# A convolution tile on GpSimd without its place behind the first norm's squares, and kept weights loaded through two buffer rings

## Chip, cores and metric

One core of a Trainium2 chip runs the whole kernel. The metric is device time in microseconds (us) of one execution; before the change the median of three runs is 753.43 us (753.04 to 754.24).

## What is computed

Two layers on a sequence of 1024 tokens of width 1024, in float32 (cut from the reference):

```
layer 0:  h = rms(x, g0) * (1 + sc) + sh
          a, b, g = split(h @ cv_w_in, 3);   y = a * sigmoid(b)
          y = depthwise_conv31(y) + db
          y = silu(layernorm(y)) * silu(g);  x = x + gt * (y @ cv_w_out)
layer 1:  h = rms(x, g1) * (1 + sc) + sh
          v, g = split(h @ pl_w_in, 2)
          y = (window_mean(v) - v) @ w_grp * scale          # four groups, windows 2, 4, 8, 16
          x = x + gt * ((y * silu(g)) @ pl_w_out)
```

`sh`, `sc` and `gt` of each layer come from `silu(c) @ w_mod`. The context prefix has no effect on the output at this depth and is left out.

## The kernel before

Everything is held transposed: 128 channels on the partitions, tokens along the free axis. The sequence is worked in two halves of 512 tokens (h = 0 and 1), the channels in eight tiles of 128 (ct = 0 to 7). Each matrix product is made from three matmuls (`mm3`, lines 217 to 219): operand and weight are each split into a rounded high part and the rest, and high times high, high times low and low times high are added. One product of a 128x1024 weight with a half is 24 matmuls of 128x512.

**How a weight arrives.** `load_split` (L193) loads 512 KB into a buffer of the ring "raw", ScalarE (ACT) writes the high part (L166), VectorE (DVE) or GpSimd (POOL) the low part (L171); both parts go to two buffers of the ring "w" unless slots are named. A raw buffer is free again as soon as the low part is written. Both rings have four buffers of the same size (L63). While layer 0's gates are computed, `split_ahead` (L557) splits twelve weights of layer 1 ahead of time and writes both parts to DRAM (`keep`, L204). Later `load_kept` (L210) brings the two parts back, as two loads of 512 KB straight into two "w" buffers, with no splitting; these buffers are free again only when the product that reads them is done. The kept weights are used in the order wv2, wv3, wq2, wq3, wv4, wv5, wq4, wq5, wv6, wv7, wq6, wq7 by the groups g = 1 to 3 of the first half of layer 1 (`layer1_group`, L737; the names in the trace end in 0 for the first half, as wv40). All loads and stores are issued by one engine (SP), in one order.

**The convolution.** `conv(h, ct)` (L483) runs 31 taps per channel tile. For five tiles of the second half (1, 3, 5, 6, 7) POOL does it: ACT writes the middle tap into z (L504), and for each further tap ACT scales the input into one of two "pr" buffers (L507) and POOL adds it to z (L508), 30 additions for a tile. The other tiles run on DVE (L520). Convolutions have a late priority, so that they fill idle time.

**Order.** The instructions of an engine run in the order in which they stand in its queue. This order is made when the program is built, by a planner that simulates the engines: of what is ready in its simulation it issues what has the best priority, and a buffer of a ring goes to the waiting request of the best priority. Program order is the priority, shifted by `LATER` for convolutions (late) and for the norms' small steps (early). `behind([i])` adds one constraint: what is written inside it on the engine of `i` is issued after `i`.

**Around the change.** `layernorm(0)` sums the first half's z on TensorE (PE), subtracts the mean, and squares each tile on ACT (L297); `squared[0]` is the last of these squares. Then come `gate_norm(0)` and `out_half(0)`, which ends layer 0 for the first half, `h2_half(0)`, and the groups of layer 1. Beside them POOL and DVE work on the second half's convolution, whose result `layernorm(1)` sums with the "mr" matmuls (L579). The conv calls read:

```
conv(1, 1)
with behind([squared[0]]):
    conv(1, 3)
conv(1, 2)
```

and `conv(1, 4)` to `conv(1, 7)` follow in the first group of layer 1 (L853).

Of the kernel before, what the change touches and what calls it, by code (L numbers as in the profile page):

```python
# [10 lines left out]
F32R = mybir.dt.float32r  # L11
# [44 lines left out]
def hybrid_kernel(ctx, tc, xT, vecs, wm, wk, cv_first, cv_w, cv_wo, pl_w, pl_grp, pl_wo, out):  # L56
# [12 lines left out]
    @contextmanager  # L69
    def priority(shift):  # L70
        base = tc.cur_priority
        tc.cur_priority = base + shift
        yield
        tc.cur_priority = base
# [6 lines left out]
    def unit(tag, name, dt=F32, cols=1024):  # L81

        width = WIDTH.get(tag[0], 1024)
        return S.tile([P, width], dt, tag=tag, name=name, bufs=RINGS.get(tag, 1))[:, :cols]
# [98 lines left out]
    @contextmanager  # L183
    def behind(instructions):
        with ExitStack() as stack:
            for i in instructions:
                stack.enter_context(tc.issue_after(i.ins))
            yield
# [15 lines left out]
    def keep(name, u):  # L204

        kept[name] = [DR.tile([P, 1024], F32, name=f"{name}{c}") for c in "hl"]
        for d, t in zip(kept[name], u):
            nc.sync.dma_start(out=d, in_=t.bitcast(F32))

    def load_kept(name, which):  # L210
        u = unit("w", which + "h", F32R), unit("w", which + "l", F32R)
        for t, d in zip(u, kept[name]):
            nc.sync.dma_start(out=t.bitcast(F32), in_=d)
        return u
# [268 lines left out]
    def conv(h, ct, taps=None, count=None):  # L483

        with priority(LATER * (1 + h)):
            for _ in islice(taps or conv_taps(h, ct), count):
                pass

    def conv_taps(h, ct):
        y = ys[ct]  # L490
        p = [ct in q for q in PAIRS].index(True)
        if (h, p) not in zu:
            zu[h, p] = unit(("Z0", "Z1", "Z2", "Z3", "Y8", "Y9", "Y0", "Y1")[4 * h + p], f"z{h}{p}")
        z = zs[h][ct] = zu[h, p][:, hs(PAIRS[p].index(ct))]

        def dw(k):
            return vcol(ct, V_DW + k)

        order = [MID, MID - 1] + [k for k in range(TAPS) if k not in (MID, MID - 1)]
        if ct in POOL_CT[h]:  # L500
            for k in order:
                o, i = span(h, k)
                if k == MID:
                    nc.scalar.activation(z, y[:, i], AF.Identity, scale=dw(k), bias=vcol(ct, V_DB))  # L504
                else:
                    pr = half("pr", f"pr{h}{ct}{k}")
                    nc.scalar.activation(pr[:, o], y[:, i], AF.Copy, scale=dw(k))  # L507
                    nc.gpsimd.tensor_tensor(out=z[:, o], in0=z[:, o], in1=pr[:, o], op=ALU.add)  # L508
                yield
            return  # L510
        acc = [bank("cv", f"cv{h}{ct}{j}") for j in range(2)]
        for n, k in enumerate(order):
            o, i = span(h, k)
            a = acc[n % 2]
            if n < 2:
                nc.vector.tensor_scalar(a[:, o], y[:, i], dw(k), None, ALU.mult)
                if o.start:
                    nc.vector.memset(a[:, : o.start], 0.0)
            else:
                nc.vector.scalar_tensor_tensor(  # L520
                    out=a[:, o], in0=y[:, i], scalar=dw(k), in1=a[:, o], op0=ALU.mult, op1=ALU.add
                )
            yield
        nc.scalar.activation(z, acc[0], AF.Identity, bias=vcol(ct, V_DB))  # L524
        nc.vector.tensor_tensor(out=z, in0=z, in1=acc[1], op=ALU.add)  # L525
# [43 lines left out]
    sums_done, squared = [None, None], [None, None]  # L569
# [103 lines left out]
    gate_g(CORD[3], (1,), [rb_done], HOLD[0], wg_last[CORD[3]])  # L673
    y1, done = gate_norm(0, z, rb)
    conv(1, 1)
    with behind([squared[0]]):
        conv(1, 3)
    conv(1, 2)
    x1, total = out_half(0, y1, ws, done)

# [51 lines left out]
    def load_pl(i, name, part):  # L732
        if part == 0 and f"kw{i}" in kept:
            return load_kept(f"kw{i}", name)
        return load_split(pl_w[i], name, eng=nc.gpsimd if part and i % KT > 1 else nc.vector)
# [195 lines left out]
```

## Time and profile before

| | before |
|---|---|
| median of 3 runs | 753.43 us (753.04 to 754.24) |
| the profiled execution's own time | 754.87 us |
| its span, first to last instruction | 753.0 us |
| PE busy | 719.6 us (96%) |
| DVE, POOL, ACT busy | 511.9, 456.9, 387.3 us (68, 61, 51%) |
| mean granted TensorE clock | 0.986 of full speed |

The span lies inside the execution's own time; 1.87 us are outside it. "Busy" is time in which an instruction of the engine runs. A line of waits gives engine, line, and what it waited for, then the total in us, the number of waits and the longest. A line of the timeline gives start and duration in us, engine, line, operation, output<-input, shapes and a count of instructions merged into it; in brackets stands the idle time before it and what ended that.

### The profile page before, as it was taken

The numbers are of one execution on the slowest core, as the hardware profiler recorded it, in microseconds if no ns is written. First come the engines' busy times: TensorE is split into PE (matmuls) and PEld (weight loads), VectorE is DVE, ScalarE is ACT, GpSimd is POOL, SyncE is SP. The second block draws the span as 40 slices with busy tenths as digits, with TensorE's granted clock in tenths as the row PEclk, the third lists the DMA queues.
The fourth block names the chain that finished last, engine by engine and source line by source line (L and its number), as shares of the span: only waits on it lengthen the run. The fifth ranks groups of instructions, "written<-read, shape, count | busy, mean of one in ns | idle before, by whom it ended". The sixth has DMA issues, their size and how long they took to land.

```text
span 753.0 us, 9988 instructions
## 1 busy us (share of the span) xinstructions
PE 719.6 (96%) x3574; PEld 568.3 (75%) x3574; DVE 511.9 (68%) x712; ACT 387.3 (51%) x577; POOL 456.9 (61%) x389
## 2 busy tenths in 40 slices
PE   3899999999999999999989979999999999999998
PEld 1677787676776788888677748777887888888997
DVE  6997998889998851589779975461737364477321
ACT  5355556656654556976876665453424433334110
POOL 2000889999986858899989997644108423343231
PEclk8899999999999999999999999999999999999999
DMA  8882006466789963643560643643726510234132
GB/s 324 314 323 82 0 1 251 160 232 236 281 346 320 372 249 111 209 141 112 195 222 31 223 169 117 218 161 133 228 91 218 187 57 28 98 113 140 57 128 72
DMA packets 43394, 130.86 MB, mean 174 GB/s; under 512 B 4816, under 2 KB 6992, under 8 KB 43344
## 3 DMA queue, kind: packets, MB, share of 16 engines
q1 hardware_dynamic: 43344, 130.22, 48.9%
q8 instruction: 28, 0.46, 0.2%
q14 instruction: 22, 0.18, 0.1%
HBM read 105.04 MB, written 25.17 MB: 173 GB/s over the span
## 4 chain that ended last, share of the span: by engine, by line
PE 71%; DVE 10%; POOL 10%; ACT 4%; issue 3%; DMA 2%; SPq 0%; POOLq 0%; DVEq 0%; ACTq 0%
POOL z L508 9%; PE ps L217 4%; PE ps L219 4%; PE ps L218 4%; PE psf L218 4%; PE psf L219 4%; PE psf L217 4%; PE psv L219 3%; PE psv L218 3%; PE psv L217 3%; PE psq L218 3%; PE psg L219 3%; PE psq L219 3%; PE psq L217 3%; PE psg L217 3%; PE psg L218 3%
## 5 line engine op out<-in xcount | busy, mean ns | idle before, releaser
L508 POOL TENSOR_TENSOR z<-z,pr 128x512 f32<-128x512 f32 (+8 forms) x210 | 292.6, 1394 | 39.0 <-ACT z L504 14.9
L507 ACT ACTIVATE pr<-y,VT 128x512 f32<-128x512 f32 (+8 forms) x210 | 150.0, 720 | 101.8 <-POOL z L508 96.3
L520 DVE SCALAR_TENSOR_TENSOR cv<-y,VT,cv 128x512 f32<-128x512 f32 (+9 forms) x261 | 175.5, 742 | 0.3
L800 DVE SCALAR_TENSOR_TENSOR q<-psy,VT,q 128x260 f32<-128x260 f32 (+1 forms) x24 | 13.6, 570 | 41.0 <-PE psy L219 40.9
L817 DVE SCALAR_TENSOR_TENSOR xf<-psf,gt,xf 128x260 f32<-128x260 f32 (+1 forms) x24 | 13.2, 570 | 38.1 <-PE psf L219 33.9
L264 POOL TENSOR_TENSOR vrx<-vex,mhalf 128x4 f32<-128x4 f32 x2 | 2.0, 1024 | 56.8 <-ACT vex L262 56.8
L609 DVE TENSOR_TENSOR z<-z,rbz 128x512 f32<-128x512 f32 x16 | 10.7, 678 | 26.0 <-PE rbz L270 26.0
L713 DVE TENSOR_TENSOR s<-v 128x535 f32<-128x535 f32 x8 | 12.3, 1539 | 19.5 <-ACT v L766 19.5
L717 DVE TENSOR_TENSOR s<-s 128x517 f32<-128x517 f32 (+5 forms) x24 | 23.1, 963 | 0.6
L323 DVE SCALAR_TENSOR_TENSOR wmb<-wmb,s_row 128x1024 f32<-128x1024 f32 x16 | 19.3, 1216 | 0.0
L166 ACT CAST y<-q 128x504 fp32r<-128x504 f32 (+1 forms) x16 | 9.9, 618 | 18.3 <-DVE q L800 18.3
L711 DVE TENSOR_TENSOR s<-v,psv 128x512 f32<-128x512 f32 x8 | 5.5, 682 | 20.3 <-ACT v L766 20.3
L335 PE MATMUL gv<-wk,srep 128*32 128x256 f32 x256 | 18.6, 388 | 0.0
L601 ACT ACTIVATE gn<-z,VT 128x512 f32<-128x512 f32 x16 | 12.3, 775 | 11.7 <-DVE z L609 11.6
L625 DVE SCALAR_TENSOR_TENSOR xr<-pso,gt,xr 128x512 f32<-128x512 f32 x16 | 11.6, 742 | 8.9 <-PE pso L219 8.9
L766 ACT COPY v<-psv 128x512 f32<-128x512 f32 x16 | 9.3, 578 | 13.3 <-PE psv L219 13.2
L171 DVE TENSOR_TENSOR y<-q,y 128x504 fp32r<-128x504 f32 (+1 forms) x16 | 13.1, 825 | 3.6 <-ACT y L166 3.6
L218 PE MATMUL psy<-pd,grs 128*128 128x260 f32 (+1 forms) x48 | 15.3, 320 | 0.0
L219 PE MATMUL psy<-pd,grs 128*128 128x260 f32 (+1 forms) x48 | 15.3, 319 | 0.0
L217 PE MATMUL psy<-pd,grs 128*128 128x260 f32 (+1 forms) x48 | 15.1, 318 | 0.0
L726 POOL TENSOR_TENSOR s<-s,ecol 128x1 f32<-128x1 f32 (+5 forms) x14 | 5.4, 384 | 15.5 <-DVE s L717 14.2
L525 DVE TENSOR_TENSOR z<-z,cv 128x512 f32<-128x512 f32 x9 | 6.2, 683 | 12.6 <-ACT z L524 12.6
(2509 smaller groups left out, 2367.2 us busy)
## 6 DMA issues: line engine op xcount, KB each, us to landing
wk<-in_wk SPq DMA_DIRECT2D x32, 512.0 KB, 5.4
wmb<-in_wm SPq DMA_DIRECT2D x16, 512.0 KB, 6.3
wo<-in_cv_wo SPq DMA_DIRECT2D x16, 512.0 KB, 3.6
wp<-in_pl_wo SPq DMA_DIRECT2D x16, 512.0 KB, 3.4
wk<-in_pl_w SPq DMA_DIRECT2D x12, 512.0 KB, 6.0
wg<-in_cv_w SPq DMA_DIRECT2D x12, 512.0 KB, 5.5
x<-in_xT SPq DMA_DIRECT2D x16, 256.0 KB, 6.3
w<-in_cv_first SPq DMA_DIRECT2D x8, 512.0 KB, 5.9
```

Of the source, the lines that this page charges most:

```text
L171: return eng.tensor_tensor(out=lo, in0=src, in1=hi.bitcast(F32), op=ALU.subtract)
L217: nc.tensor.matmul(ps, w[0], r[0], start=first, stop=False)
L218: nc.tensor.matmul(ps, w[0], r[1], start=False, stop=False)
L219: nc.tensor.matmul(ps, w[1], r[0], start=False, stop=last)
L323: nc.vector.scalar_tensor_tensor(out=w, in0=w, scalar=1.0, in1=s_row, op0=ALU.mult, op1=ALU.mult, accum_out=out)
L335: nc.tensor.matmul(ps[32 * q : 32 * q + 32, :256], srep[:, kt, :], w[:, 256 * q : 256 * q + 256], start=kt == 0, stop=kt == KT - 1,)
L507: nc.scalar.activation(pr[:, o], y[:, i], AF.Copy, scale=dw(k))
L508: nc.gpsimd.tensor_tensor(out=z[:, o], in0=z[:, o], in1=pr[:, o], op=ALU.add)
L520: nc.vector.scalar_tensor_tensor(out=a[:, o], in0=y[:, i], scalar=dw(k), in1=a[:, o], op0=ALU.mult, op1=ALU.add)
L717: nc.vector.tensor_tensor(out=s[:, :m], in0=s[:, :m], in1=s[:, step : step + m], op=ALU.add)
L800: mixed[0] = nc.vector.scalar_tensor_tensor(out=sg[m][:, piece], in0=ps, scalar=vcol(ct, V_PS), in1=sg[m][:, piece], op0=ALU.mult, op1=ALU ...
L817: nc.vector.scalar_tensor_tensor(out=xt[:, piece], in0=ps, scalar=gt1[:, m : m + 1], in1=xt[:, piece], op0=ALU.mult, op1=ALU.add)
```

## The change

The constraint on `conv(1, 3)` is taken away, so that its ACT steps (and with them POOL's additions) may be planned before the first norm's squares. And `load_kept` takes its two buffers from the rings "w" and "raw" in turn: wv2, wq2, wv4, wq4, wv6, wq6 from "w", wv3, wq3, wv5, wq5, wv7, wq7 from "raw".

```diff
+    loaded = []
+
     def load_kept(name, which):
-        u = unit("w", which + "h", F32R), unit("w", which + "l", F32R)
+        tag = ("w", "raw")[len(loaded) % 2]
+        loaded.append(name)
+        u = unit(tag, which + "h", F32R), unit(tag, which + "l", F32R)
         for t, d in zip(u, kept[name]):
             nc.sync.dma_start(out=t.bitcast(F32), in_=d)
         return u
...
     conv(1, 1)
-    with behind([squared[0]]):
-        conv(1, 3)
+    conv(1, 3)
     conv(1, 2)
```

## Rows read from the trace of the kernel before

**Rows 1.** The page, part 1: busy time and share of each engine.
```profile
PE 719.6 (96%) x3574; PEld 568.3 (75%) x3574; DVE 511.9 (68%) x712; ACT 387.3 (51%) x577; POOL 456.9 (61%) x389
```
**Rows 2.** Windows: stretch, length; busy PE, PEld, DVE, ACT, POOL; clock, DMA share, GB/s.
```profile
220.20:284.80 64.60, 63.63 (x303) 49.91 (x302) 47.98 (x76) 31.93 (x42) 42.83 (x19) 1.00 0.84 306
...
360.00:390.00 30.00, 26.25 (x116) 19.93 (x115) 19.99 (x17) 22.67 (x37) 28.10 (x17) 1.00 0.56 185
...
426.00:444.60 18.60, 16.04 (x64) 11.17 (x62) 17.17 (x22) 12.14 (x19) 18.06 (x20) 1.00 0.50 183
444.60:455.20 10.60, 6.37 (x15) 4.75 (x16) 2.18 (x4) 6.42 (x10) 10.16 (x12) 0.68 0.58 225
455.20:486.50 31.30, 31.30 (x136) 25.21 (x134) 17.54 (x20) 16.75 (x27) 23.95 (x28) 1.00 0.51 170
486.50:740.00 253.50, 253.02 (x1343) 211.76 (x1343) 127.52 (x164) 90.18 (x132) 92.29 (x71) 1.00 0.38 128
```
**Rows 3.** Waits of PE over the whole span.
```profile
PE psv L217 <- DMA wv40h<-kw4h: 2.6, 1, 2.6
PE psv L219 <- DMA wv40l<-kw4l: 1.6, 1, 1.6
...
PE mr L579 <- POOL z L508: 1.2, 1, 1.2
...
PE psq L219 <- DMA wq20l<-kw10l: 0.7, 1, 0.7
PE psq L217 <- DMA wq20h<-kw10h: 0.7, 1, 0.7
...
PE psg L219 <- POOL wg60l L171: 0.5, 1, 0.5
```
**Rows 4.** Timeline of PE, 420 to 487 us.
```profile
420.47 0.39 PE L219 MATMUL psv<-h206h,wv20l 128*128 128x512 f32 x1
...
438.65 0.39 PE L219 MATMUL psq<-h206h,wq20l 128*128 128x512 f32 x1
...
450.13 0.63 PE L217 MATMUL psv<-h200h,wv40h 128*128 128x512 f32 x1
...
455.25 0.43 PE L217 MATMUL psv<-h204h,wv40h 128*128 128x512 f32 x1
...
486.50 1.05 PE L579 MATMUL mr<-z,onesd 128*32 128x512 f32 x4
```
**Rows 5.** Timeline of SP's queue, 425 to 444 us: start and duration of each issue.
```profile
425.64 0.38 SPq L213 DMA_DIRECT2D wq20h<-kw10h  x1
...
439.59 0.32 SPq L595 DMA_DIRECT2D sgr<-sgd  x1
...
443.10 0.36 SPq L213 DMA_DIRECT2D wv40h<-kw4h  x1
```
**Rows 6.** Waits of SP's queue, 400 to 450 us.
```profile
SPq L595 <- DVE cv L520: 12.0, 1, 12.0
...
SPq L196 <- DVE grs L171: 2.7, 1, 2.7
```
**Rows 7.** DMA issues, 440 to 460 us: median us from issue to landing.
```profile
wv40l<-kw4l SPq DMA_DIRECT2D x1, 512.0 KB, 5.9
...
wv50l<-kw5l SPq DMA_DIRECT2D x1, 512.0 KB, 8.2
```
**Rows 8.** Line L504 of ACT in its timeline, 283.3 us.
```profile
283.30 0.80 ACT L504 ACTIVATE z<-y,VT 128x512 f32<-128x512 f32 x1
```
**Rows 9.** Timeline of POOL, 233 and 271 us; in brackets the idle time before.
```profile
233.26 2.42 POOL L171 TENSOR_TENSOR wk12l<-wk,wk12h 128x1024 fp32r<-128x1024 f32 x1 [4.74 <-ACT wk12h L166]
...
271.30 2.41 POOL L171 TENSOR_TENSOR wg10l<-wg,wg10h 128x1024 fp32r<-128x1024 f32 x1 [8.30 <-PE psg L219]
```
**Rows 10.** Line L508, 284.5 to 484.5 us: count, ns min/median/max, first and last start.
```profile
L508 POOL TENSOR_TENSOR z<-z,pr x120: 1247/1293/2372, 284.8 to 482.8; 128x512 f32<-128x512 f32 x60, 128x511 f32<-128x511 f32 x4, 128x510 f32<-128x510 f32 x4, 128x509 f32<-128x509 f32 x4
```
**Rows 11.** Waits of ACT, 284.5 to 484.5 us.
```profile
ACT pr L507 <- POOL z L508: 43.8, 62, 2.4
```

## The prediction

> **What bounds the kernel now.** PE is busy 719.6 us of a span of 753.0 [rows 1], so this is a kernel bound by PE, and an edit that moves work of POOL and loads can only win what PE loses: its idle time and its time at a low clock. The busy shares say no more, so I read next where PE stands still. In windows [rows 2] the reader is to see three stretches. From 360 to 390 us PE is idle for 30.00 - 26.25 = 3.75 us. From 426 to 444.6 it is idle for 2.56 us, and from 444.6 to 455.2 for 4.23 us, with the clock at 0.68 in the mean. From 455.2 on it is full: 31.30 of 31.30, then 253.02 of 253.50.
>
> The waits [rows 3] say who is late. In the second and third stretch it is the loads of two kept weights, wq2 (0.7 + 0.7 us) and wv4 (2.6 + 1.6 us), and one addition of the convolution on POOL (the mr matmul, 1.2 us). The timeline [rows 4] shows what the clock cost: from 450.13 to 455.25 there are twelve matmuls of 0.427 us from start to start, where the full stretch after 455.2 has 31.30 us for 136, 0.23 each [rows 2]. That is the lower level of 1.2 GHz after two gaps in which PE stood, and it costs 12 x 0.196 = 2.35 us.
>
> Why were the loads late? wv4 takes the "w" buffers that wq2 gives back with its last matmul at 438.65 + 0.39 = 439.0 us [rows 4]. Its load was issued at 443.10 [rows 5]. In front of it in SP's queue stood a gate's reload, which waited 12.0 us for a DVE convolution, and a wo load, which waited 2.7 us for a raw buffer that DVE had to release [rows 6]. Its low part then took 5.9 us to land [rows 7]. So the queue cost 4.1 us and the ring the rest: with two weights in four buffers a load can't start before the last product but one has ended. wq2 has the same story: its buffers were free at 420.9 [rows 4], the load was issued at 425.64 [rows 5].
>
> **Kept weights in two rings.** Added and removed bytes: none; the same 24 loads of 512 KB. What changes is which release each waits for. wq2 gets the second pair of "w" buffers, free since the last gate weight was used, so it can be loaded with wv2 some 25 us ahead; wv4 takes wv2's buffers, free at 420.9, some 24 us before PE wants it at 444.6. Both waits go: 0.7 + 0.7 + 2.6 + 1.6 = 5.6 us. With no gap there the clock stays up: 2.35 us more.
>
> The other six kept weights now hold raw buffers until their product is over, not only until a split. Behind them in the ring are the group weights (gr), the four wp weights of the output product and the wo weights. In the trace of before a raw request delayed by this is not to be seen. Their cover: the wp weights are read only around 500 us, and the wo weights later still. If the cover is gone, the price is a wait as that of wv4. wv5 is the tight one: it needs two raw buffers that come back from wv3's successors (a wp and a gr split by DVE) or from wq3. Bounds: nothing, if it lands under wv4's product, and 2.6 + 1.6 + 2.35 = 6.55 us, the whole price of wv4. I take 0.7 us, wq2's wait, the nearest row: a load a little late with nothing standing in front of it.
>
> **POOL's tile set free.** Of conv(1, 3), 30 additions on POOL and as many scalings on ACT are neither added nor removed, only allowed earlier. It began at 283.30 [rows 8], behind the last square. From 220.2 to 284.8 POOL is busy 42.83 of 64.60 us [rows 2], idle 21.8, in a few gaps (4.74 and 8.30 us the largest [rows 9]). An addition takes 1.293 us in the median [rows 10]: the two gaps hold 3 + 6, all the idle time 16. I take 13, so POOL's chain of four tiles, 120 additions from 284.8 to 484.1 [rows 10], ends about 13 x 1.29 = 17 us earlier.
>
> The Trainium skill (SBUF — State Buffer, Who interferes with whom) says that GpSimd and a DVE instruction with two SBUF inputs exclude each other for a whole instruction. Additions of up to 2.372 us [rows 10] fit that; in this stretch DVE mostly runs taps with one input in PSUM, so by the rule 1.29 holds, and at 2.37 the idle time would take 9 additions and the lead would shrink to 12 us by the median; the sum would not move.
>
> What is 17 us on POOL worth? Not 17: PE is full from 455 on, so an earlier layernorm(1) meets no idle PE. It is worth the 1.2 us that the first mr waits, and it pays for something that the first edit brings. If PE is no longer held at 444.6, it comes to the next mr not at 486.50 [rows 4] but 4.2 + 2.35 = 6.55 us earlier, at 479.95, while POOL's last addition ends at 482.8 + 1.27 = 484.1 [rows 10]: a new wait of 4.1 us. With the lead of 17 us it could vanish. But the mr matmuls stand in PE's queue where the planner's clock puts them, and it will move them forward with POOL's planned end; whether real POOL is late against real PE remains. Bounds: 0, and 4.1 + 1.4 = 5.5 us, if their relative places stay as they are (the 1.4 of wq2 comes back at the first mr in the same way). I take 2.4: two mr groups, each waiting the 1.2 us of the one that was seen.
>
> What the early additions disturb: in this stretch POOL also writes the low parts of the gate weights, and PE already waits 0.5 us for one (wg60l [rows 3]), so there is no slack there. One addition in front of such a split delays it by 1.29. Bounds: 0, if the planner fits them into real gaps, and three gate weights in a row, 3.9. I take 1.3. ACT's scalings wait for POOL to release a pr buffer (62 waits, 43.8 us, at most 2.4 [rows 11]); the norm's squares queue behind them on ACT, and gate_norm(0) behind those. PE's cover there is the products of two gates; I take nothing, and 2.4 us as the other bound. The 3.75 us from 360 to 390 are ACT and DVE splits behind additions; another tile's additions will stand there, so nothing is gained.
>
> **Sum.** Removed: 5.6 + 2.35 + 1.2 = 9.15. Added: 0.7 + 2.4 + 1.3 = 4.4. Net -4.75 us. The profiled execution took 754.87 us in all, so 750.1 for a like one; the median of the runs is 1.44 us lower, and 753.43 - 4.75 = **748.7 us**.
>
> **Rivals.**
> - *POOL becomes the bound of the stretch (no change).* The new waits at the mr groups come in full, 5.5 us, one of them long enough to drop the clock as at 450 (2.35), and 1.3 is lost early: 9.15 - 9.15 = 0, 753.4 us. For it: POOL is busy 18.06 of 18.60 us there. Against: the lead of 17 us. That the planner leaves conv(1, 3) where it was, for want of idle time in its simulation, belongs here too.
> - *The raw ring takes over the wait (slower).* Raw buffers held for a whole product put a gr, wp or wo load in SP's single queue in front of a kept load, and wv5, and after it wq5 or wv7, come as late as wv4 did. It decides from the point at which a raw weight is issued after its predecessor's product and lands later than the 5.5 us of the product between. wv5's low part took 8.2 us to land [rows 7], so this can be. Two such waits with their clock are 13.1 us against the 9.15 removed, and 1.3 early: 753.4 + 5.2 = 758.6 at full price, some 757 if the second drops no clock.
> - *Nothing is given back (faster still).* 9.15 whole and a part of the 3.75 because POOL's tiles fall otherwise: 742 to 744.
>
> **How the numbers follow.** Forecast 0.50, its own range 746 to 751.5; no change 0.17; slower 0.21; faster still 0.12. A measurement here tells about 0.2% (1.5 us) from no change. All of the last, and nearly all of the forecast, are faster: 0.60. Same 0.17, slower 0.23. The range, 743.0 to 757.0, reaches into both outer cases.
>
> **What would show it.** Right: no PE wait on a DMA of a kept weight; wq2's load issued near wv2's; clock 1.00 around 450; additions between 220 and 284; layernorm(1) some 15 us earlier. The give-back shows as PE's waits mr <- POOL. Wrong: PE waits for wv5, wq3 or a wp weight; SP's queue waiting for a product to release a raw buffer; PE waits for gate splits or squares between 226 and 300; or a PE order so different that other gaps open after 455, where I count none.

## The result and the profile after

The changed kernel takes 744.89 us in the median of four runs (744.55 to 746.58), the kernel before 753.84 us beside it on the same chip (753.04 to 755.82): a ratio of 0.9882, with a 95% interval of 0.9857 to 0.9907. Two later comparisons gave 0.9888 [0.9867, 0.9908] and 0.9881 [0.9865, 0.9898]. So it is 8.9 us faster, where 4.75 were forecast: inside the range of 743.0 to 757.0, below the forecast's own 746 to 751.5. The profiled execution took 746.58 us, the longest of the four, with a span of 744.8 us against 753.0 before. In the changed kernel the lines stand 3 or 4 further down (the products at L221 to L223, POOL's addition at L512, the mr matmul at L583).

First the page's part 1 of the changed kernel, beside [rows 1]:

```profile
PE 718.7 (96%) x3574; PEld 568.7 (76%) x3574; DVE 506.1 (68%) x712; ACT 386.6 (52%) x577; POOL 452.4 (61%) x389
```

PE's busy time fell by only 0.9 us; its idle time fell from 753.0 - 719.6 = 33.4 to 26.1 us. Where, the windows say (the columns are those of [rows 2]; the stretch from 390 to 426 stands here for both kernels). The changed kernel:

```profile
220.20:284.80 64.60, 63.29 (x301) 49.53 (x301) 47.97 (x76) 40.05 (x56) 62.14 (x34) 1.00 0.83 299
360.00:390.00 30.00, 26.33 (x116) 19.62 (x114) 19.03 (x16) 22.43 (x36) 28.77 (x17) 1.00 0.68 229
390.00:426.00 36.00, 34.89 (x141) 25.65 (x142) 35.58 (x48) 25.97 (x40) 34.22 (x39) 0.95 0.17 59
426.00:444.60 18.60, 18.60 (x83) 15.15 (x82) 15.31 (x19) 13.39 (x21) 17.87 (x22) 1.00 0.60 218
444.60:455.20 10.60, 10.60 (x46) 7.73 (x45) 2.78 (x4) 3.78 (x7) 6.80 (x9) 1.00 0.72 260
455.20:486.50 31.30, 31.30 (x186) 23.82 (x184) 18.16 (x28) 11.86 (x21) 2.00 (x10) 1.00 0.43 154
```

The kernel before, 390 to 426 us:

```profile
390.00:426.00 36.00, 35.96 (x155) 27.23 (x155) 34.35 (x45) 25.73 (x39) 33.46 (x35) 1.00 0.32 117
```

The 2.56 and 4.23 us in which PE stood from 426 to 455.2 [rows 2] are gone, and so is the clock of 0.68 there. New are 1.11 us of idle PE after 390, with a clock of 0.95 in the mean, and 0.34 us more before 284.8, where POOL is now busy 62.14 of 64.60 us instead of 42.83. POOL is nearly done by 455 (2.00 us in the next stretch, 23.95 before).

PE's waits from 220 to 500 us in the changed kernel, beside [rows 3]:

```profile
PE psg L223 <- DVE wg51l L171: 1.4, 1, 1.4
PE psv L221 <- ACT h200h L167: 1.3, 1, 1.3
PE psg L223 <- POOL wg60l L171: 1.1, 1, 1.1
PE psv L222 <- DVE h200l L172: 0.7, 1, 0.7
...
PE psg L223 <- POOL wg50l L171: 0.2, 1, 0.2
```

No wait for a kept weight is left, and none for an mr matmul. wg60l rose from 0.5 to 1.1 us, and wg50l is new with 0.2. What I had not foreseen is a wait for the two parts of h200, the first slice of layer 1's input. Two waits that the list of before had in the same stretch are gone:

```profile
PE psg L219 <- DVE wg71l L171: 0.8, 1, 0.8
...
PE psg L217 <- ACT wg50h L166: 0.5, 1, 0.5
```

The loads, in SP's timeline of the changed kernel (beside [rows 5]):

```profile
384.94 0.42 SPq L217 DMA_DIRECT2D wv20h<-kw2h  x1
...
388.96 0.32 SPq L217 DMA_DIRECT2D wq20h<-kw10h  x1
...
424.42 0.37 SPq L217 DMA_DIRECT2D wv40l<-kw4l  x1
430.16 0.32 SPq L599 DMA_DIRECT2D sgr<-sgd  x1
...
441.50 0.32 SPq L217 DMA_DIRECT2D wv50l<-kw5l  x1
```

And its DMA issues from 424 to 446 us (last number: median us from issue to landing):

```profile
wv40l<-kw4l SPq DMA_DIRECT2D x1, 512.0 KB, 4.5
...
wv50l<-kw5l SPq DMA_DIRECT2D x1, 512.0 KB, 5.5
```

wq2's load left 4.0 us behind wv2's, as expected, and wv4's at 424 instead of 443. Its low part took 4.5 us to land and was there at 428.9, 14.5 us before PE began the product at 443.42. wv5 was the tight one: its low part left at 441.50, took 5.5 us, and was first read at 449.43, so 2.4 us were to spare.

The end of POOL's chain, in its timeline (the last addition of before ended at 484.1 [rows 10]):

```profile
446.78 3.95 POOL L512 TENSOR_TENSOR z<-z,pr 128x499 f32<-128x499 f32 x3
```

It ends at 450.7, 33.4 us earlier.

The same matmul's start in both profiled executions shows how the gain builds up:

| matmul | before | after | difference |
|---|---|---|---|
| first of the products that read h200 (psv<-h200h,we00h) | 390.29 | 390.44 | +0.15 |
| second psv<-h204h,we00l, some 10 us later | 399.90 | 403.24 | +3.34 |
| psq<-h204h,wq20h | 436.00 | 435.10 | -0.90 |
| second psv<-h204h,wv40h | 455.25 | 446.88 | -8.37 |
| the last product's psf<-y,wp60h | 595.60 | 587.38 | -8.22 |

Of the +3.34, 1.15 is five matmuls of the products with we20 and we30, which stand ahead of this point in PE's queue now and stood behind it before (44 matmuls from the first row to this one instead of 39); it comes back in the next row. The rest of that row's 4.24 is the waits for wq2 and mr (2.6 us) and 0.5 us more, since by the start times a stop costs more than the wait listed for it. From 455 on nothing more is won and 0.15 lost.

### The profile page after: what moved, and what is told of

The parts are those of the page before. It is cut to its first block, busy times and chain, and to the rows that moved or that the text cites. A ratio compares the mean times of both kernels' runs of the same rounds, so it can differ in the third digit from the quotient of the medians.

```text
span 744.8 us, 9979 instructions
## 1 busy us (share of the span) xinstructions
PE 718.7 (96%) x3574; PEld 568.7 (76%) x3574; DVE 506.1 (68%) x712; ACT 386.6 (52%) x577; POOL 452.4 (61%) x389
## 4 chain that ended last, share of the span: by engine, by line
PE 73%; POOL 10%; DMA 7%; DVE 5%; ACT 2%; issue 2%; SPq 0%; POOLq 0%; DVEq 0%; ACTq 0%
POOL z L512 9%; PE psv L223 4%; PE psv L222 4%; PE psf L223 4%; PE psf L221 4%; PE psq L223 4%; PE psf L222 4%; PE psv L221 4%; PE psq L222 4%; PE psq L221 4%; PE ps L221 3%; PE ps L223 3%; PE ps L222 3%; PE psg L223 3%; PE psg L221 2%; PE psg L222 2%
## 5 line engine op out<-in xcount | busy, mean ns | idle before, releaser
L512 POOL TENSOR_TENSOR z<-z,pr 128x512 f32<-128x512 f32 (+8 forms) x210 | 292.0, 1392 | 35.0 <-ACT z L508 14.9
L720 DVE TENSOR_TENSOR s<-s 128x517 f32<-128x517 f32 (+5 forms) x24 | 17.5, 731 | 0.6
L223 PE MATMUL psy<-pd,grs 128*128 128x260 f32 (+1 forms) x48 | 15.3, 319 | 0.0
L221 PE MATMUL psy<-pd,grs 128*128 128x260 f32 (+1 forms) x48 | 15.2, 320 | 0.0
```

What stands on the lines that cost most here:

```text
L221: nc.tensor.matmul(ps, w[0], r[0], start=first, stop=False)
L223: nc.tensor.matmul(ps, w[1], r[0], start=False, stop=last)
L720: nc.vector.tensor_tensor(out=s[:, :m], in0=s[:, :m], in1=s[:, step : step + m], op=ALU.add)
```

## Experiments

The theory with which I went in: the rings bring the gain; the free tile brings nothing by itself and gives the rings back what POOL would else hold up. First the halves alone, the changed kernel again beside them, and conv(1, 3) put later.

**e1_rings_only: the rings without the free tile.**

```diff
     conv(1, 1)
-    conv(1, 3)
+    with behind([squared[0]]):
+        conv(1, 3)
     conv(1, 2)
```

> Kept weights in two rings, conv(1, 3) behind the first norm's squares as before. Theory (the rings remove the waits for kept weights, POOL's lead keeps them from coming back at the mr matmuls): the waits for wq2 and wv4 (5.6 us) and the low clock (2.35 us) are gone, but PE now meets POOL's late z: mr <- POOL waits of 4 to 5.5 us in all, net 2.5 to 4 us faster than before. Rival A (the rings are the whole gain, POOL's tile is idle baggage): 8 us faster or more, mr <- POOL no longer than the 1.2 us of before. Rival B (POOL's tile is the whole gain, its earlier end clears SP's queue): at most 2 us faster, wv4 still waited for.

Measured: 747.19 us (746.09 to 749.05, six runs), ratio 0.9922 [0.9899, 0.9945], so 6.4 us faster: more than the theory's 2.5 to 4, less than rival A's 8. PE's waits from 380 to 500 us are one line:

```profile
PE mr L583 <- POOL z L512: 1.6, 1, 1.6
```

The kept weights are on time without the free tile. The give-back, which I had put at 2.4 us with the free tile, is there at 1.6 us without it, and at nothing with it. h200 is not waited for.

**e2_conv_only: the free tile with the kept weights in one ring.** The edit is the removed `with behind([squared[0]])` in the kernel before, and no other.

> conv(1, 3) free, kept weights all in the ring w as before. Theory: mr <- POOL (1.2 us) is gone, the waits for kept weights (some 5.6 us) and the low clock (2.35 us) stay, the first product on h2 waits some 2 us and drops the clock (together 3.5 us) as in the changed kernel; net from 1 us faster to 3 us slower. Rival A: slower by 2 to 4 us, the new wait at h2 being all that this edit brings. Rival B: 6 us faster or more, wv4 issued by 440 us and no wait for it.

Measured: 753.77 us (752.73 to 755.06, twelve runs), ratio 1.0005 [0.9992, 1.0018]: no difference. PE's waits from 380 to 500 us:

```profile
PE psv L217 <- DMA wv40h<-kw4h: 3.4, 1, 3.4
PE psv L218 <- DVE h200l L172: 0.7, 1, 0.7
PE psq L219 <- DMA wq20l<-kw10l: 0.4, 1, 0.4
PE psv L219 <- DMA wv40l<-kw4l: 0.4, 1, 0.4
...
```

The wait of 1.2 us for POOL [rows 3] is gone. PE comes to wv4 1.2 us earlier than before (446.83 - 3.44 against 447.20 - 2.62), but its load lets it start only 0.4 us earlier; of the two waits for wv4 the first grew from 2.6 to 3.4 us and the second fell from 1.6 to 0.4. The load sets the time there, and a wait for h200l, 0.7 us, is new. POOL's chain ends at 455.8, 28.3 us earlier.

**e3_after_again: the changed kernel, beside these.**

> The changed kernel once more, beside the two halves on one chip, to add them up: 8.5 to 9.5 us faster than before. If the halves add up, e1 and e2 sum to this; theory: their sum falls short of it by 3 us or more, since each takes away what limits the other; rival A: they add up within 1.5 us.

Measured: 744.87 us (744.67 to 745.2, five runs), ratio 0.9888 [0.9867, 0.9908]. Against the shared 753.63 us of the kernel before, the halves are -6.4 and +0.1, and together they are -8.8: 2.5 us more than their sum. I had expected their sum to fall short of the whole by 3 us or more: the direction was right, the size was not reached; the rival, that they add up within 1.5 us, missed. The free tile is worth something only once the loads no longer set the time: the 1.6 us that PE waits for POOL in e1 are gone here, and the runs of e1 and e3 do not meet. The account is not closed. The free tile also brings the wait for h200, and e1's six runs lie in two groups, 746.1 to 746.4 and 748.0 to 749.1 us; its trace is of the first. Against that group the free tile gains 1.4 us, against e1's median 2.3.

**e4_conv_later: the other direction.** In e1, conv(1, 3) is put behind the end of the gate norm:

```diff
-    with behind([squared[0]]):
+    with behind(done[:1]):
         conv(1, 3)
```

> Kept weights in two rings, and conv(1, 3) held back further, behind gate_norm(0)'s last SiLU on ACT (near 321 us instead of 283): POOL starts its chain of four tiles some 35 us later. Theory: POOL's end is then what layernorm(1) waits for; the planner puts mr later too, but PE runs out of other work: mr or vpz waits of 5 us or more, and slower than e1 by 5 to 15 us. Rival A (POOL's place does not matter as long as PE has other work): within 2 us of e1.

Measured: 769.0 us (767.2 to 769.6), ratio 1.0204 [1.0181, 1.0227], 21.8 us above e1, more than I expected. Its waits of PE from 290 to 600 us, and a window (columns as before):

```profile
PE mr L583 <- POOL z L512: 4.6, 2, 2.5
PE rbz L274 <- ACT dgz L273: 2.8, 1, 2.8
PE vpz L318 <- ACT sqz L316: 2.6, 4, 1.7
PE pso L221 <- ACT wo17h L166: 2.1, 1, 2.1
...
520.00:560.00 40.00, 31.15 (x162) 20.13 (x161) 18.89 (x30) 19.63 (x33) 15.08 (x12) 0.79 0.47 159
```

In e1 PE is busy 40.00 of 40.00 us in that window, at full clock. A POOL that is late does not cost its one wait: the second norm comes late, PE waits for its short steps too (rbz, vpz), as no long product is left to cover them, and the clock goes down to 0.79 in the mean. So a later place of the tile costs much more (21.8 us) than the earlier one gains (2.3 us, e3 against e1). Where between the places of e1 and e4 it turns steep was not tried.

The second batch asks what is left (the wait for h200) and what made the loads late (SP's queue, or the ring).

**e5_conv6_16 and e6_conv6_14: less of POOL's work ahead of h200.** In the changed kernel ACT's scalings for conv(1, 6) from its 17th addition on (15th in e6), and all of conv(1, 7), are put behind ACT's first high part of h2 (h200h, kept in `h2_hi`):

```diff
+    h2_hi = []
...
-                hi_part(res[kt][0], x, sh1[:, kt : kt + 1])
+                hi = hi_part(res[kt][0], x, sh1[:, kt : kt + 1])
+                if kt == 0:
+                    h2_hi.append(hi)
...
-                for ct in range(4, KT):
-                    conv(1, ct)
+                conv(1, 4)
+                conv(1, 5)
+                taps = conv_taps(1, 6)
+                conv(1, 6, taps, 17)
+                with behind(h2_hi[:1]):
+                    conv(1, 6, taps)
+                    conv(1, 7)
```

> The changed kernel, with the later taps of conv(1, 6) (from the 17th addition on) and conv(1, 7) put on ACT behind the first high part of layer 1's input (h200h). In the changed kernel h200h's input is there near 385 us, but ACT does it only at 389.7, because scalings for POOL stand in front of it and wait for a pr buffer; PE waits 1.3 and 0.7 us and then runs 8 to 9 matmuls at the low clock (1.6 to 1.8 us). Theory (the new wait is ACT's order, and POOL has time to spare): those 2 us of waits go and the clock stays up, 2 to 3.5 us faster than the changed kernel; POOL ends some 4 us later without a wait for it. Rival (the wait is the length of the norm's chain, or POOL has no time to spare): within 1 us of the changed kernel, or slower with mr <- POOL back.

> As the kernel before it, two additions earlier (from the 15th on). Theory: the first high part comes still earlier by up to 1.5 us, same gain within 1 us; POOL idles some 3 us more. Rival: slower than the kernel before it by 2 us or more, as the additions held back reach mr.

Measured: 743.31 us (741.95 to 744.01, ratio 0.9873 [0.985, 0.9896]) and 743.4 us (742.18 to 743.71, ratio 0.9872 [0.9847, 0.9897]). In both PE waits for nothing from 380 to 490 us, neither for h200 nor at an mr matmul. The changed kernel was not in this batch, so I ran both side by side.

**e9_conv6_beside and e10_after_beside: that version and the changed kernel on one chip.**

> The kernel of e5 again, now beside the changed kernel on one chip. Theory (ScalarE's queue held the high half of h2 up; about 3.5 us of new waits and low clock, of which some is given back): 743.3 us, 1.0 to 2.5 below the changed kernel measured beside it, and no wait for h200h or h200l. Rival (the two batches' chips differed and the late h2 costs nothing at the end): within 0.5 us of the changed kernel, though its waits are gone.

> The changed kernel, unaltered, as the other side of that comparison. Both: 744.9 us within 0.7, with the waits of 1.3 for h200h and 0.7 for h200l. If it comes out near 743.5, e5's lead was the chip's and not the edit's.

Measured: 743.17 us (742.35 to 744.02) and 744.83 us (744.56 to 745.42), four runs each; the ranges don't meet. The ratios to the same runs of before are 0.9859 [0.9844, 0.9874] and 0.9881 [0.9865, 0.9898]. So the late h200 costs 1.7 us of the end time, and its cause is the order on ACT. (In e10's own profile PE waits 0.7 us for h200l and not at all for h200h, which I had expected too; the last section says why.) ACT's timeline in the changed kernel (the run profiled first), and DVE's, which makes h200's input xr:

```profile
384.97 0.73 ACT L511 ACTIVATE pr<-y,VT 128x509 f32<-128x509 f32 x1 [0.99 <-POOL z L512]
386.33 0.72 ACT L511 ACTIVATE pr<-y,VT 128x508 f32<-128x508 f32 x1 [0.64 <-POOL z L512]
...
389.06 0.72 ACT L511 ACTIVATE pr<-y,VT 128x506 f32<-128x506 f32 x1 [0.64 <-POOL z L512]
389.68 1.32 ACT L167 ACTIVATE h200h<-xr,sh 128x512 fp32r<-128x512 f32 x2
```

```profile
384.10 1.41 DVE L660 SCALAR_TENSOR_TENSOR xr<-xr,a,rby 128x512 f32<-128x512 f32 x2 [0.31 <-PE rby L274]
```

and in e9:

```profile
385.09 0.72 ACT L167 ACTIVATE h200h<-xr,sh 128x512 fp32r<-128x512 f32 x1 [1.04 <-DVE xr L662]
```

In e9 ACT waits for h200's own input from DVE and then starts. In the changed kernel scalings stand in front in ACT's queue, each waiting for POOL to release a pr buffer, and h200 comes 4.6 us later than in e9, though both slices of its input were there at 385.5.

**e7_kept_act_queue: SP's queue taken out.** In the kernel before, the kept loads are issued by ACT:

```diff
         for t, d in zip(u, kept[name]):
-            nc.sync.dma_start(out=t.bitcast(F32), in_=d)
+            nc.scalar.dma_start(out=t.bitcast(F32), in_=d)
```

> The kernel before, with the loads of kept weights issued from ACT's queue instead of SP's; one ring, conv(1, 3) as before. Theory (of the 4.2 us that PE waits for wv4, most is SP's queue, not the ring): wv4's load is then issued near 439 to 440 us when wq2's product ends, PE waits at most 1.5 us for it, and the low clock is gone: 3 to 6 us faster, unless ACT, which waits for POOL in between, issues late itself. Rival (two weights in four buffers are too few whatever the queue): the waits for wv4 stay at 3 us or more, within 2 us of before.

Measured: 752.64 us (750.57 to 754.58, ten runs), ratio 0.9992 [0.9973, 1.0011]: no difference, where the theory had 3 to 6 us. PE's waits from 380 to 500 us, and DMA issues from 438 to 462 us (last number: median us from issue to landing):

```profile
PE psv L217 <- DMA wv40h<-kw4h: 2.2, 1, 2.2
PE psq L217 <- DMA wq20h<-kw10h: 2.0, 1, 2.0
...
sgr<-sgd SPq DMA_DIRECT2D x1, 512.0 KB, 7.4
wv40h<-kw4h ACTq DMA_DIRECT2D x1, 512.0 KB, 7.4
wv40l<-kw4l ACTq DMA_DIRECT2D x1, 512.0 KB, 8.2
```

and in the kernel before:

```profile
wv40h<-kw4h SPq DMA_DIRECT2D x1, 512.0 KB, 4.0
```

wv4's load now leaves at 441.5 instead of 443.10, right after its buffers are free (wq2's last matmul ends at 441.3 here). Its high part lands no earlier, at 448.9 instead of 447.1: it goes together with the sgr load, which no longer stands in front of it, and each takes 7.4 us, where they took 4.0 and 3.3 in the trace of before. For wq2 the run takes no queue away, it only changes it: ACT waits for POOL in between and issues wq2's load at 427.44, SP did at 425.64 [rows 5]. The Trainium skill (DMA: Bandwidth & Descriptors, Issuing engines are not separate DMA queues) says that loads started by different engines run on the same DMA engines and interleave, so that a second issuing engine saves only the time of issuing; that fits these two landings.

**e8_raw_only: one ring again, the other one.** In the changed kernel all twelve kept weights go to "raw":

```diff
-        tag = ("w", "raw")[len(loaded) % 2]
+        tag = "raw"
```

> The changed kernel with all kept weights in the ring raw: again two weights in four buffers, shared with the gr, wp and wo loads. Theory (it is the number of weights in flight that pays, and raw buffers held for a product are a price that the changed kernel escapes only because half of the weights use w): waits for kept weights of 5 us or more in all with a clock drop, 6 to 15 us slower than the changed kernel. Rival (the ring's identity does not matter as long as the load need not wait for the last product but one): within 3 us of the changed kernel.

Measured: 760.22 us (759.06 to 761.29), ratio 1.0098 [1.0069, 1.0127], 15.3 us above the changed kernel, at the upper end of what I expected. PE's waits, SP's longest, and a window:

```profile
PE psv L221 <- DMA wv40h<-kw4h: 6.9, 1, 6.9
PE psv L221 <- DMA wv60h<-kw6h: 1.4, 1, 1.4
...
SPq L217 <- PE psv L223: 50.6, 4, 27.5
...
444.60:455.20 10.60, 6.75 (x16) 4.89 (x17) 1.84 (x2) 1.77 (x3) 5.57 (x5) 0.52 0.67 248
```

So it is not the other ring that helps, but both together: two weights in flight wait in either ring (the kernel before, e8), four in two rings do not (e1). Four in one ring were not tried. The raw ring is the worse one to fill: SP's queue, where the other loads stand too, waits 50.6 us for products here.

## Why the prediction was right, and where it was off

**The removed part, 9.15 us, held.** wq2's and wv4's waits, the low clock at 450 and the mr wait are gone from the list and the windows. From 436 to 455 the start of the same matmul gains 7.5 us, where wv4's 2.6 + 1.6 and the clock's 2.35 make 6.55. Of the other 0.9, some 0.4 is one more slow matmul in front of the twelve I counted (0.59 us from start to start, 449.54 to 450.13); the rest is time at the stops that the list of waits does not count.

**The cause of the late loads was half wrong.** "So the queue cost 4.1 us and the ring the rest", said of wv4, does not stand as a price: e7 takes SP's queue from wv4's load and wins nothing. With four buffers the load still can't start before wq2's product ends, and what it gains in front it loses in landing beside the load that it has passed; wq2, which ACT now issues, is waited for 2.0 us instead of 1.4. Kept weights in both rings are what helps (e1, e8); how much of the lateness was the queue's alone, no run separates.

**wv5's 0.7 us were 0.** The raw ring did not take over the wait; 2.4 us were to spare. One sign that was named as wrong did come: SP's queue waits for a product to release a raw buffer (L196 loads into one; the kernel before has no such wait from 380 to 500 us), only no wait of PE follows from it.

```profile
SPq L196 <- PE psv L223: 9.1, 2, 4.6
```

e8 shows that this rival's mechanism exists, and that with half of the weights the kernel stays clear of it.

**The give-back of 2.4 us was the term that failed.** It measured 1.6 us in e1 and 0 in the changed kernel. I had the mechanism (a lead of POOL pays for what the rings bring), and did not draw its consequence: the lead of 17 us was already more than the 5.5 us that it had to pay for. I kept 2.4 because real POOL might be late against the mr matmuls, which the planner moves forward with it. It was not: the last mr matmul starts at 454.1, behind POOL's end at 450.7. I also made the lead too short: 13 additions at 1.293 us. The trace has 16 additions before 284.8, as many as the prediction had for all of the idle time:

```profile
L512 POOL TENSOR_TENSOR z<-z,pr x16: 1270/1294/1319, 222.5 to 284.0; 128x512 f32<-128x512 f32 x14, 128x511 f32<-128x511 f32 x1, 128x510 f32<-128x510 f32 x1
```

and each is worth not its own length but its share of the later stretch, in which POOL does other work too: 199.3 us for 120 additions [rows 10], 1.66 each, 26.6 us for 16. Measured were 28.3 us for the free tile alone (e2); the rings alone bring 5.9 (the chain ends at 478.2 in e1). So the last mr matmul of layernorm(1) came 33 us earlier (487.0 before), where some 15 were named. The longest of the early additions took 1.319 us. By the rule of the Trainium skill (SBUF — State Buffer, Who interferes with whom) DVE work with one of its two inputs in PSUM leaves GpSimd alone; the trace agrees, with 1.294 us in the median of this row.

**The early price of 1.3 us was about 0.8**: wg60l 0.6 more and wg50l 0.2 (together 0.4 and 0.6 in the profiles of e3 and e10). The waits for wg71l (0.8 us) and wg50h (0.5 us) went, which I had not counted, so the stretch to 390 was no loss.

**Not foreseen: h200.** "Another tile's additions will stand there, so nothing is gained" from 360 to 390 was said of the sum of the gaps, and I took ACT's queue at nothing with a bound of 2.4, at the norm's squares. It was in this queue, but at h200: PE came to it 1.13 us earlier than before (390.44 - 1.28 against 390.29) and ACT 1.1 us later (389.68 against 388.59). PE waited 1.28 + 0.67 us. In this one execution the clock fell as well, eight matmuls in 3.39 us where full clock needs 1.84:

```profile
390.44 0.50 PE L221 MATMUL psv<-h200h,we00h 128*128 128x512 f32 x1 [1.28 <-ACT h200h L167]
...
392.31 0.56 PE L222 MATMUL psv<-h200l,we00h 128*128 128x512 f32 x1 [0.67 <-DVE h200l L172]
392.68 0.63 PE L223 MATMUL psv<-h200h,we00l 128*128 128x512 f32 x1
...
396.07 0.39 PE L222 MATMUL psq<-h200l,we30h 128*128 128x512 f32 x1
```

**The sum.** Removed 9.15 as said; added 0.8 less wg71l's 0.8, no wv5, no give-back, and 1.7 at h200 by e9 against e10: 7.5, where 8.9 were measured. The stops at wv4 and those at wq2 and mr cost 0.9 and 0.5 us more than was counted for them, and wg50h's 0.5 went as well: 9.4, and the half microsecond too much I can put to no row. So the forecast's mechanism decided, but the time lies nearer to the rival "nothing given back" (742 to 744): the give-back was nothing, and it is h200's wait that keeps the time 1 us above that rival. Without that wait (e9) the kernel lies inside the rival's interval. The range held because it reaches into this rival; the forecast's own 746 to 751.5 was missed by 1.1 us. (The "some 757" of the slower rival is 756.3 by its own terms, 758.6 - 2.35; nothing hangs on it.)

Open: why e1's runs lie in two groups some 2 us apart where the changed kernel's mostly keep within 1. More than two weights in flight in the "w" ring itself were not tried, so the number in flight and the second ring are not told apart.

## What to carry to other kernels

A buffer that is held until its product is over allows only as many loads ahead as there are buffers: count weights in flight before you look at the queue in front of the load, and look for a ring that is idle in that stage. Work moved forward on a helper engine is worth nothing while another wait sets the time, and can become worth its price when that wait goes; so try such edits together, and price the lead by what the engine does per step in the stretch that gets shorter. Then look at who shares the helper's feeder: here ACT's in-order queue made a critical cast wait 4.6 us behind scalings for POOL, and putting those behind the cast gave another 1.7 us (743.17 us, the best version here).

## Not expected of the hardware

The clock's fall after a gap is not the same from one execution to the next. The changed kernel waits 1.4 us for wg51l at 377 and 0.7 us for h200l at 392 in all three of its profiles (the first, e3's and e10's), and 1.3 us for h200h at 390 in the first and in e3's. In the first profile:

```profile
375.00:380.00 5.00, 3.53 (x14) 2.62 (x15) 4.93 (x3) 3.67 (x8) 4.71 (x4) 1.00 0.45 157
390.00:396.50 6.50, 5.39 (x15) 3.98 (x16) 6.08 (x7) 5.47 (x9) 5.70 (x8) 0.74 0.76 278
```

in that of e10:

```profile
375.00:380.00 5.00, 3.39 (x8) 2.46 (x9) 4.79 (x3) 3.80 (x8) 4.71 (x3) 0.71 0.47 156
390.00:396.50 6.50, 5.73 (x24) 4.06 (x23) 5.96 (x6) 5.59 (x9) 5.70 (x8) 1.00 0.82 301
```

The granted clock falls at 390 in the one (0.74) and at 377 in the other (0.71), and in e3's profile in neither window (1.00 in both). In e10's the fall comes ahead of h200h: PE is later by it, and does not wait for h200h. Those executions took 746.58, 745.10 and 744.67 us, and a fall costs some 1.55 us here (the 3.39 - 1.84 above); so a cost that one profile shows in clock need not be in the median.
